# A hybrid decoder step on one core: the one-hot table loaded as 96 rows and one, the key-value state shifted memory to memory

## The chip, the core and the metric

The kernel runs on one core of a Trainium2 chip. The time is what the device reports for one execution, in microseconds (us). The kernel before took 3317.05 us, the median of three runs (3311.76 to 3326.76). The profiled execution from which every row below is taken took 3318.74 us.

Five engines have instruction streams of their own: TensorE (PE, with PEld for its weight loads), VectorE (DVE), ScalarE (ACT), GpSimd (POOL) and SyncE (SP). SP computes nothing here; it issues most of the DMAs. ACT and POOL issue some as well. The transfers themselves run on 16 DMA engines, and a DMA share of 1.00 in the profile means that all 16 are busy.

## The reference, cut to what matters

One step of a decoder layer for a prompt of 1024 tokens and for 8 decode samples. Each token passes a state-space branch and a sparse attention branch, then a mixture of 32 experts. The change touches two places: the bias of the attention by distance, and the sliding-window attention of the 8 samples.

```python
def attend_shared(q, k, v, q_pos, k_pos, mask, table):
    s = jnp.einsum('bhgqd,bkhd->bhgqk', q, k).astype(F32) * HEAD_DIM ** -0.5
    s = s + shared_bias(table, q_pos[:, None] - k_pos[None, :])    # table[rel_bucket(distance)]
    ...
def nsa_sample(...):
    ...
    wkv = jnp.concatenate([win_buf, kv_win], 1)        # 512 old rows and the new one
    ...                                                # attend_window(q, wkv, ...)
# outputs
win_s.append(jnp.concatenate([state_win_kv[l], kvw], 1)[:, -state_win_kv.shape[2]:])
```

`state_win_kv` holds, for each of 8 samples, 512 rows of 256 floats: 128 of keys and 128 of values. The output `win_s` is the same buffer moved up by one row, with the new row at the end; so 511 rows of each sample (523,264 bytes) go from input to output unchanged. The one-hot table `k_onehot` is a constant of 97 rows by 4224 columns in bfloat16 (8448 bytes a row), with which TensorE turns the 32 bias buckets into a bias for each distance.

## The kernel before

The kernel is one program in stages. From 0 to about 430 us the **front** interleaves four strands by a string of letters (ORDER): adaLN (`r`, 24 steps; each loads 1 MB of `w_ada` into one of two `wt` buffers at L499 and multiplies it at L504), the compression of the samples' paged cache (`c`, L1141 to L1166, whose transposes are L1155 and whose products are L475 to L477), the state-space tables (`S`) and the bias tables (`B`, `bias_prep`). Then come the input projections, from about 703 us the prompt attention, from about 1205 us the output projection and routing, from about 1400 us the experts, and from about 3218 us the combination.

**bias_prep** loads the one-hot table `oh` with one DMA from SP's queue (L1240). Its products with the bias table (L1246 to L1271) give the bias for the prompt (`bt`, spread to `bx` by L1250), for the selected blocks, the window and the compressed blocks.

**The prompt attention** (`attention`) walks over 2 head groups and 8 blocks of 128 queries. Between its pieces it takes steps of a second chain, `sample_attention`, at 0.9 steps to a piece; both chains share the in-order queues of PE, DVE and ACT, so a sample step that waits holds up the prompt's work behind it.

**The window part of sample_attention** (L1679 to L1735) takes the samples one by one. `fetch` (L1685) loads a whole 512 KB state with SP into one of two `slab` buffers. For each sample SP stores the slab, moved by a row, to `win_s`: three rows from one partition (L1694) and 508 rows from 127 partitions (L1695). DVE copies the values into `wv` (L1696), PE transposes the keys (L1699), ACT evicts them (L1702), PE multiplies them with the queries (L1705). The buffer of sample b is free for sample b + 2 when its stores have landed. The pool of these tiles opens when the part before it, the selected blocks, has let go of its own: its last reader is L1674.

What sets the order of instructions around the change is a scheduler of the tile framework: within a stage it places each instruction on its engine's queue by the dependencies and by its own estimate of when they are met; the queues are then in order on the chip. DMAs from SP and ACT share eight completion semaphores in turn, and a DMA waits at issue until the earlier one with the same semaphore is done.

Of the kernel before, what the change touches and what calls it, by code (L numbers as in the profile page):

```python
# [10 lines left out]
F = mybir.dt.float32  # L11
# [12 lines left out]
B = 8  # L24
# [426 lines left out]
class K:  # L451
# [763 lines left out]
    def bias_prep(self):  # L1215
        nc, tc, i = self.nc, self.tc, self.i
# [5 lines left out]
        with ExitStack() as c:  # L1222
            p = self.pool("bp", ctx=c)
            q = self.pool("bpq", bufs=2, psum=True, ctx=c)

            tf = p.tile([97, 8], F, name="tf")
            nc.vector.memset(tf[96:97], NEG)
            for k in range(3):
                nc.sync.dma_start(out=tf[32 * k:32 * k + 32], in_=i["rel_bias"])
            tb = p.tile([97, 8], BF, name="tb")  # L1230
            nc.vector.tensor_copy(out=tb, in_=tf)
            t1 = p.tile([96, 8], F, name="t1")
            nc.vector.tensor_tensor(out=t1, in0=tf[0:96], in1=tb[0:96], op=ALU.subtract)
            t2 = p.tile([96, 8], BF, name="t2")
            nc.vector.tensor_copy(out=t2, in_=t1)
            nc.vector.tensor_tensor(out=t1, in0=t1, in1=t2, op=ALU.subtract)
            nc.vector.tensor_copy(out=tb[32:64], in_=t2[32:64])
            nc.vector.tensor_copy(out=tb[64:96], in_=t1[64:96])
            oh = p.tile([97, 4224], BF, name="oh")
            nc.sync.dma_start(out=oh, in_=i["k_onehot"])  # L1240
            bv = p.tile([8, 1152], F, name="bv")
            nc.vector.memset(bv, NEG)
            for a in range(0, 1151, 512):
                n = min(512, 1151 - a)
                po = q.tile([128, 512], F, name="po")[:8]
                nc.tensor.matmul(po[:, :n], lhsT=tb, rhs=oh[:, 3073 + a:3073 + a + n], start=True, stop=True)  # L1246
                nc.vector.tensor_copy(out=bv[:, a:a + n], in_=po[:, :n])
            nc.sync.dma_start(out=self.bt, in_=bv)

            nc.sync.dma_start(out=self.bx, in_=self.bt[:, None].to_broadcast([8, 128, 1152]))  # L1250

            ps = q.tile([128, 512], F, name="po")[:, :256].rearrange("p (a j h) -> p a j h", a=4, j=8)
            for a in range(4):
                for j in range(8):
                    nc.tensor.matmul(ps[:, a, j], lhsT=oh[:, a * 1024 + j:(a + 1) * 1024:8], rhs=tb, start=True, stop=True)
            bs = p.tile([128, 2, 4, 8, 4], F, name="bs")
            for h in range(2):
                nc.vector.tensor_copy(out=bs[:, h], in_=ps[:, :, :, h * 4:h * 4 + 4])
            nc.sync.dma_start(out=self.bsel.rearrange("h a p f -> p h a f"), in_=bs.rearrange("p h a j g -> p h a (j g)"))
            pw = q.tile([128, 512], F, name="po")[:, :32].rearrange("p (j h) -> p j h", j=4)  # L1260
            for j in range(4):
                nc.tensor.matmul(pw[:, j], lhsT=oh[:, 3584 + j:4096:4], rhs=tb, start=True, stop=True)
            bw = p.tile([128, 4, 8], F, name="bw")
            nc.vector.tensor_copy(out=bw, in_=pw)
            nc.sync.dma_start(out=self.bwin, in_=bw)
            t8 = p.tile([97, 8, 8], BF, name="t8")
            nc.vector.tensor_copy(out=t8, in_=tb[:, None, :].to_broadcast([97, 8, 8]))
            pc = q.tile([128, 512], F, name="po")[:64, :256]
            t8 = t8.rearrange("p a b -> p (a b)")
            nc.tensor.matmul(pc[:, 0:255], lhsT=t8, rhs=oh[:, 31:4096:16], start=True, stop=True)  # L1270
            nc.tensor.matmul(pc[:, 255:256], lhsT=t8, rhs=oh[:, 4096:4097], start=True, stop=True)  # L1271
            bc = p.tile([64, 256], F, name="bc")
            nc.vector.tensor_copy(out=bc, in_=pc)
            nc.sync.dma_start(out=self.bcmp, in_=bc)
# [327 lines left out]
    def sample_attention(self, bank):  # L1602
        nc, tc, i = self.nc, self.tc, self.i
        v, A, pe, g_ = nc.vector, nc.scalar, nc.tensor, nc.gpsimd
        self.atts = tc.dram_tile([128, 4, B], F, name="atts")
        lo, hi = half = (slice(0, 64), slice(64, 128))
        ident, keep = self.ident, self.keep
# [4 lines left out]
        with ExitStack() as c:  # L1612
            p = self.pool("sa", ctx=c, side="right")
# [3 lines left out]
            def fetch(k):  # L1617
                w = p.tile([120, 8, 256], F, name="slab", bufs=2)
                g_.indirect_dma_start(out=w.rearrange("p j f -> p (j f)"), out_offset=None, in_=pool, in_offset=off(ap=self.rx[:, 0, k:k + 1], axis=0))
                sb = p.tile([120, 8, 4], F, name="sb", bufs=2)  # L1620
                g_.indirect_dma_start(out=sb.rearrange("p j g -> p (j g)"), out_offset=None, in_=btab, in_offset=off(ap=self.rx[:, 1, k:k + 1], axis=0))
                return w, sb
# [6 lines left out]
            ahead = fetch(0)  # L1629
            ahead += (keys(ahead[0], 0),)  # L1630
            for n in range(4):
                sv = p.tile([120, 4, 8, 64], F, name="sv")
                st = p.tile([120, 8, 4, 4], F, name="st")
                for k in range(4):
                    b, h = divmod(4 * n + k, 2)
                    (w, sb, kw), ahead = ahead, fetch(4 * n + k + 1) if 4 * n + k < 15 else None
                    g_.tensor_copy(out=sv[:, k], in_=w[:, :, 128 + 64 * h:192 + 64 * h])
                    tp = bank(128, 4, 128)
# [13 lines left out]
                for j0 in (0, 4):  # L1652
                    tp = bank(16, 4, 128)
# [24 lines left out]
        with ExitStack() as c:  # L1678
            p = self.pool("saw", ctx=c, side="right")  # L1679
            wv = p.tile([128, B, 4, 128], F, name="wv")  # L1680
# [2 lines left out]
            nc.sync.dma_start(out=bw, in_=self.bwin)  # L1683

            def fetch(b):  # L1685
                w = p.tile([128, 4, 256], F, name="slab", bufs=2)
                nc.sync.dma_start(out=w, in_=i["state_win_kv"][0, b].rearrange("(p j) c h d -> p j (c h d)", j=4))
                return w

            ahead = fetch(0)  # L1690
            for b in range(B):
                w, ahead = ahead, fetch(b + 1) if b < B - 1 else None
                wo = self.o["win_s"][0, b].rearrange("t c h d -> t (c h d)")
                nc.sync.dma_start(out=wo[0:3].rearrange("(p j) f -> p j f", j=3), in_=w[0:1, 1:4])  # L1694
                nc.sync.dma_start(out=wo[3:511].rearrange("(p j) f -> p j f", j=4), in_=w[1:128])  # L1695
                v.tensor_copy(out=wv[:, b], in_=w[:, :, 128:256])  # L1696
                tp = bank(128, 4, 128)
                for j in range(4):
                    pe.transpose(tp[:, j], w[:, j, 0:128], ident)  # L1699
                yield  # L1700
                kt = p.tile([128, 4, 128], F, name="kt")
                A.activation(out=kt, in_=tp, func=AF.Copy)  # L1702
                ws = bank(128, 4, 8)
                for j in range(4):
                    pe.matmul(ws[:, j], lhsT=kt[:, j], rhs=self.qk[:, b], start=True, stop=True)  # L1705
                yield
                v.tensor_tensor(out=wsb[:, :, b], in0=ws, in1=bw, op=ALU.add)
            pw = p.tile([64, 528], F, name="pw")
            tp = bank(64, 4, 128)
# [27 lines left out]
        with ExitStack() as c:  # L1737
            p = self.pool("sac", ctx=c, side="right")
# [577 lines left out]
```

## Time and profile before

| | |
|---|---|
| median of 3 runs | 3317.05 us (3311.76 to 3326.76) |
| profiled execution | 3318.74 us |
| its span | 3316.9 us, so 1.84 us lie around it |
| PE busy | 2963.7 us, 89% |
| DVE busy | 2319.3 us, 70% |
| ACT busy | 1785.9 us, 54% |
| POOL busy | 347.4 us, 10% |
| moved by DMA | 656.34 MB, mean 198 GB/s |

The shares are means over stages with different limits. In the page's line of PE by slices (40 slices of 83 us) a 9 is a slice in which PE hardly rests; the slices to look at are those without. PE idle time counts as waiting when the row names a releaser: "<-DMA slab" means that PE stood until that transfer had landed. PEclk is the clock granted to TensorE, as a share of full speed: 1.00 is 2.4 GHz and 0.50 is 1.2 GHz. DMA is the share of 16 engines, so one engine working alone reads 0.06.

### The profile page before, as it was taken

The page shows a single profiled execution, that of the slowest core. Times are in us where ns is not written, and L with a number is a line of the kernel's source. Part 1 is how long each engine was busy: PE and PEld are TensorE (multiplying, and loading weights), DVE is VectorE, ACT ScalarE, POOL GpSimd, SP SyncE. Part 2 cuts the span into 40 slices and gives each one's busy share as a digit, 9 for nine tenths or more (in the row PEclk, how much of TensorE's full clock was granted, in tenths as well). Part 3 has the DMA queues.
Part 4 walks back from the last instruction along what each step waited for, and adds up shares of the span by engine and source line. Part 5 has one row for each costly group of instructions (what it writes and reads, how often), then busy time and mean ns, then how long its engine had stood idle before and what let it go on. Part 6 is the DMA issues. An engine that isn't in the chain of part 4 may idle for free. (4 is left out here: it accounts for less than half of the span.)

```text
span 3316.9 us, 51065 instructions
## 1 busy us (share of the span) xinstructions
PE 2963.7 (89%) x15681; PEld 2374.8 (72%) x15682; DVE 2319.3 (70%) x4442; ACT 1785.9 (54%) x2824; POOL 347.4 (10%) x451
## 2 busy tenths in 40 slices
PE   6857899998982689769999999999999999999987
PEld 4535699976772458548788888878887888878762
DVE  4734856347871468778978877785579866697878
ACT  2422545456661364346757666574467754575752
POOL 1710121002200000000000000000000000000013
PEclk9978999998995779879999999999999999999988
DMA  7746333223411143289988988892449934694926
GB/s 254 238 164 229 136 111 111 86 72 87 117 45 50 46 161 116 106 295 305 330 279 274 316 284 281 282 319 83 149 158 371 368 125 158 212 363 144 310 96 280
DMA packets 446216, 656.34 MB, mean 198 GB/s; under 512 B 45199, under 2 KB 370816, under 8 KB 442033
## 3 DMA queue, kind: packets, MB, share of 16 engines
q1 hardware_dynamic: 420210, 539.60, 48.5%
q0 software_dynamic: 23184, 111.39, 9.9%
q10 hardware_dynamic: 2704, 3.85, 0.3%
q8 instruction: 64, 1.05, 0.1%
q14 instruction: 54, 0.44, 0.0%
HBM read 590.77 MB, written 68.73 MB: 199 GB/s over the span
## 5 line engine op out<-in xcount | busy, mean ns | idle before, releaser
L272 DVE TENSOR_TENSOR lo<-raw,hi 128x1024 fp32r<-128x1024 f32 x870 | 1030.9, 1222 | 306.9 <-ACT hi L199 301.6
L199 ACT ACTIVATE hi<-raw 128x1024 fp32r<-128x1024 f32 x870 | 916.4, 1060 | 490.6 <-PE pc L388 489.5
L386 PE MATMUL pc<-hi,X 128*128 128x512 f32 x1408 | 560.8, 398 | 4.7 <-DVE X L277 3.8
L388 PE MATMUL pc<-hi,X 128*128 128x512 f32 x1408 | 550.8, 391 | 0.0
L387 PE MATMUL pc<-lo,X 128*128 128x512 f32 x1408 | 549.9, 391 | 0.0
L386 PEld LDWEIGHTS pc<-hi,X 128*128 128x128 f32 x1408 | 265.1, 188 | 60.5 <-issue 8.9
L388 PEld LDWEIGHTS pc<-hi,X 128*128 128x128 f32 x1408 | 264.8, 188 | 56.4
L387 PEld LDWEIGHTS pc<-lo,X 128*128 128x128 f32 x1408 | 265.3, 188 | 51.5
L386 PE MATMUL pc<-hi,HT 128*128 128x512 f32 x704 | 282.7, 402 | 12.1 <-DVE HT L294 9.1
L388 PE MATMUL pc<-hi,HT 128*128 128x512 f32 x704 | 274.7, 390 | 0.0
L387 PE MATMUL pc<-lo,HT 128*128 128x512 f32 x704 | 274.6, 390 | 0.0
L386 PEld LDWEIGHTS pc<-hi,HT 128*128 128x128 f32 x704 | 132.2, 188 | 53.5 <-issue 28.6
L388 PEld LDWEIGHTS pc<-hi,HT 128*128 128x128 f32 x704 | 132.2, 188 | 28.2
L387 PEld LDWEIGHTS pc<-lo,HT 128*128 128x128 f32 x704 | 132.4, 188 | 24.7
L504 PE MATMUL po<-wt,ct 128*9 128x256 f32 x384 | 100.5, 400 | 55.3 <-DMA wt<-in_w_ada_dram 52.6
L475 PE MATMUL po<-wih,hh 128*128 128x256 f32 (+3 forms) x504 | 147.7, 293 | 0.0
L476 PE MATMUL po<-wil,hh 128*128 128x256 f32 (+3 forms) x504 | 147.0, 292 | 0.0
L477 PE MATMUL po<-wih,hl 128*128 128x256 f32 (+3 forms) x504 | 145.9, 289 | 0.0
L1318 DVE CUSTOM_DVE_ANT_0 pt<-sc,tt 128x512 f32<-128x512 f32 (+7 forms) x256 | 107.3, 436 | 52.8 <-PE sc L1334 29.7
L1157 ACT ACTIVATE xh<-tp 128x512 fp32r<-128x512 f32 x128 | 71.3, 595 | 109.2 <-PE tp L1155 101.9
L421 POOL DMA_INDIRECT xg<-hd,ic x52 | 68.2, 1311 | 586.0 <-PE px L354 554.7
L1371 PE MATMUL tp<-ident,pt 128*128 128x128 f32 (+6 forms) x592 | 115.5, 305 | 4.6 <-DVE pt L1357 4.3
(697 smaller groups left out, 5718.6 us busy)
## 6 DMA issues: line engine op xcount, KB each, us to landing
raw<-in_w_gate_up_dram SPq DMA_DIRECT2D x248, 1024.0 KB, 10.1
raw<-in_w_down_dram SPq DMA_DIRECT2D x64, 2048.0 KB
wt<-in_w_ada_dram SPq DMA_DIRECT2D x24, 1024.0 KB
yd<-yt SPq DMA_DIRECT2D x44, 512.0 KB
w<-ssmw SPq DMA_DIRECT2D x16, 512.0 KB
raw<-in_w_gate_up_dram POOLq DMA_DIRECT2D x8, 1024.0 KB, 13.7
wir<-in_w_in_dram SPq DMA_DIRECT2D x20, 256.0 KB
bx<-bt SPq DMA_DIRECT2D x1, 4608.0 KB
```

The source lines that it names most:

```text
L199: A.activation(out=hi[:,u%H],in_=rawview(u),func=AF.Copy).then_inc(S['hi'][u],1)
L272: V.tensor_tensor(out=lo[:,u%H],in0=rawview(u),in1=hi[:,u%H].bitcast(F),op=ALU.subtract).then_inc(S['lo'][u],1)
L386: PE.matmul(o,lhsT=sH,rhs=wh,start=kt==0,stop=False)
L387: PE.matmul(o,lhsT=sH,rhs=wl,start=False,stop=False)
L388: ins=PE.matmul(o,lhsT=sL,rhs=wh,start=False,stop=kt==7)
L475: pe.matmul(o, lhsT=lh, rhs=rh, start=start, stop=False)
L476: pe.matmul(o, lhsT=lh, rhs=rl, start=False, stop=False)
L477: return pe.matmul(o, lhsT=ll, rhs=rh, start=False, stop=stop)
L504: last = nc.tensor.matmul(po, lhsT=ct[:, k], rhs=wt[:, k], start=k == 0, stop=k == KT - 1)
L1157: nc.scalar.activation(out=xo, in_=tp, func=AF.Copy)
L1318: v.tensor_tensor_reduce(out=pt[:, off[r] + a:off[r] + a + n], in0=sc, in1=bias, scale=1.0, scalar=-3e38, op0=ALU.add, op1=ALU.max, accum_ ...
L1371: pe.transpose(tp[:n, h * 128:h * 128 + 128], pr[h][:, a:a + n], self.ident)
```

## The change

Two edits in the code. In `bias_prep` the one-hot table is loaded with two DMAs, rows 0 to 95 and row 96. In the window part the keys and the values are loaded by two DMAs of 256 KB each from POOL's queue, the keys into one of four `slab` buffers and the values straight into `wv`, three samples ahead; the copy on DVE is gone. The shift of the state no longer passes through the chip's memory: one DMA for each sample copies the 511 rows from the input in HBM to the output in HBM, written as 128 pieces of 4088 bytes.

```diff
             oh = p.tile([97, 4224], BF, name="oh")
-            nc.sync.dma_start(out=oh, in_=i["k_onehot"])
+            for a, b in ((0, 96), (96, 97)):
+                nc.sync.dma_start(out=oh[a:b], in_=i["k_onehot"][a:b])
 ...
             def fetch(b):
-                w = p.tile([128, 4, 256], F, name="slab", bufs=2)
-                nc.sync.dma_start(out=w, in_=i["state_win_kv"][0, b].rearrange("(p j) c h d -> p j (c h d)", j=4))
+                w = p.tile([128, 4, 128], F, name="slab", bufs=4)
+                src = i["state_win_kv"][0, b].rearrange("(p j) c h d -> p j c (h d)", j=4)
+                g_.dma_start(out=w, in_=src[:, :, 0])
+                g_.dma_start(out=wv[:, b], in_=src[:, :, 1])
                 return w
 
-            ahead = fetch(0)
+            ahead = [fetch(b) for b in range(3)]
             for b in range(B):
-                w, ahead = ahead, fetch(b + 1) if b < B - 1 else None
-                wo = self.o["win_s"][0, b].rearrange("t c h d -> t (c h d)")
-                nc.sync.dma_start(out=wo[0:3].rearrange("(p j) f -> p j f", j=3), in_=w[0:1, 1:4])
-                nc.sync.dma_start(out=wo[3:511].rearrange("(p j) f -> p j f", j=4), in_=w[1:128])
-                v.tensor_copy(out=wv[:, b], in_=w[:, :, 128:256])
+                w = ahead.pop(0)
+                if b < B - 3:
+                    ahead.append(fetch(b + 3))
+
+                flat = [d[0, b].rearrange("t c h d -> (t c h d)") for d in (self.o["win_s"], i["state_win_kv"])]
+                nc.sync.dma_start(out=flat[0][0:511 * 256].rearrange("(a f) -> a f", a=128), in_=flat[1][256:512 * 256].rearrange("(a f) -> a f", a=128))
                 tp = bank(128, 4, 128)
                 for j in range(4):
-                    pe.transpose(tp[:, j], w[:, j, 0:128], ident)
+                    pe.transpose(tp[:, j], w[:, j], ident)
```

The order moves more than the diff says. On SP's queue around the load of the one-hot table there stands before (`ssmw` is a table of the state-space part, `wt` the adaLN weights, `tf` the bias table, `bx` its spread copy):

```order
L947 DMA ssmw<-wt 128x512
L1229 DMA tf<-in_rel_bias_dram 32x8 x3
L1240 DMA oh<-in_k_onehot_dram 97x4224
L499 DMA wt<-in_w_ada_dram 128x8x256 x5
L1248 DMA bt<-bv 8x1152
L1259 DMA bsel<-bs 128x8x32
L1265 DMA bwin<-bw 128x32
L1274 DMA bcmp<-bc 64x256
L1250 DMA bx<-bt 1024x1x1152
L499 DMA wt<-in_w_ada_dram 128x8x256 x7
```

And on the same queue at the same place now:

```order
L947 DMA ssmw<-wt 128x512
L499 DMA wt<-in_w_ada_dram 128x8x256 x2
L1229 DMA tf<-in_rel_bias_dram 32x8 x3
L1241 DMA oh<-in_k_onehot_dram 96x4224
L499 DMA wt<-in_w_ada_dram 128x8x256
L1241 DMA oh<-in_k_onehot_dram 1x4224
L1700 DMA out_dram<-in_state_win_kv_dram 16x8176
L499 DMA wt<-in_w_ada_dram 128x8x256
L1700 DMA out_dram<-in_state_win_kv_dram 16x8176
L499 DMA wt<-in_w_ada_dram 128x8x256 x2
L1700 DMA out_dram<-in_state_win_kv_dram 16x8176
L1249 DMA bt<-bv 8x1152
```

The thirteenth load of `wt`, first behind the table before, now stands ahead of it. The copies of the state (L1700) wait for no computation, and so the scheduler has pulled all eight out of the window part into the front: four before the table, three here and one after `bx`. The compiler has folded the 128 pieces of each into 16 rows of 8176 floats (32,704 bytes).

On SP's queue at the start of the window part there stood before:

```order
L1683 DMA bw<-bwin 128x32
L1687 DMA slab<-in_state_win_kv_dram 128x1024 x2
L1694 DMA out_dram<-slab 1x768
L1695 DMA out_dram<-slab 127x1024
L1694 DMA out_dram<-slab 1x768
L1695 DMA out_dram<-slab 127x1024
L1687 DMA slab<-in_state_win_kv_dram 128x1024 x2
```

On POOL's queue, where the loads stand now (the first row is the last work for the selected blocks):

```order
L1627 COPY kw<-slab 120x512
L1689 DMA slab<-in_state_win_kv_dram 128x4x128
L1690 DMA wv<-in_state_win_kv_dram 128x4x128
L1689 DMA slab<-in_state_win_kv_dram 128x4x128
L1690 DMA wv<-in_state_win_kv_dram 128x4x128
L1689 DMA slab<-in_state_win_kv_dram 128x4x128
L1690 DMA wv<-in_state_win_kv_dram 128x4x128
L1689 DMA slab<-in_state_win_kv_dram 128x4x128
```

The loads and stores of the window have left SP; POOL issues 16 loads, and behind them on its queue stands nothing until the output projection. A third place is the front from about 120 to 150 us, again SP's queue; before (each `ssmw` and `ssmk` is a store that waits for DVE, ACT or POOL):

```order
L933 DMA ssmw<-v_1036 128x4x128
L927 DMA ssmw<-o_1031 128x2x512
L499 DMA wt<-in_w_ada_dram 128x8x256
L941 DMA ssmk<-kt 16x4x128
L947 DMA ssmw<-wt 128x512
```

Now:

```order
L933 DMA ssmw<-v_1036 128x4x128
L927 DMA ssmw<-o_1031 128x2x512
L1700 DMA out_dram<-in_state_win_kv_dram 16x8176
L941 DMA ssmk<-kt 16x4x128
L947 DMA ssmw<-wt 128x512
L927 DMA ssmw<-o_1068 128x2x512
L933 DMA ssmw<-v_1073 128x4x128
L941 DMA ssmk<-kt 16x4x128
L947 DMA ssmw<-wt 128x512
L933 DMA ssmw<-v_1110 128x4x128
L499 DMA wt<-in_w_ada_dram 128x8x256
```

A copy has taken the place of the ninth `wt` load, which now stands behind seven more stores.

## Rows read from the trace of the kernel before

**Rows 1.** The page's second part: PE and DMA in 40 slices, tenths.

```profile
PE   6857899998982689769999999999999999999987
DMA  7746333223411143289988988892449934694926
```

**Rows 2.** Waits of PE, 180 to 330 us: total, times, longest.

```profile
PE po L504 <- DMA wt<-in_w_ada_dram: 51.4, 2, 34.0
```

**Rows 3.** Waits of PE, 960 to 1140 us.

```profile
PE b L1699 <- DMA slab<-in_state_win_kv_dram: 95.3, 4, 33.7
```

**Rows 4.** Waits of SP's queue, 960 to 1140 us.

```profile
SPq L1687 <- DMA out_dram<-slab: 76.7, 6, 13.6
```

**Rows 5.** Stretches: us, busy PE, PEld, DVE, ACT, POOL, PEclk, DMA share, GB/s.

```profile
200.00:216.00 16.00, 0.00 (x0) 0.00 (x0) 0.00 (x0) 0.00 (x0) 0.00 (x0) 0.50 0.06 27
256.00:264.00 8.00, 8.00 (x54) 5.64 (x54) 3.77 (x8) 2.79 (x6) 1.12 (x2) 1.00 1.07 428
281.00:292.00 11.00, 9.96 (x68) 7.16 (x67) 6.53 (x12) 4.25 (x9) 1.04 (x2) 1.00 0.53 209
...
720.00:980.00 260.00, 239.13 (x1505) 188.04 (x1504) 202.86 (x787) 172.43 (x409) 52.14 (x64) 0.90 0.33 80
980.00:1135.00 155.00, 58.88 (x293) 48.09 (x293) 40.07 (x158) 37.52 (x85) 0.00 (x0) 0.64 0.13 48
```

**Rows 6.** DMA issues: count, KB each, median us to landing where known.

```profile
bx<-bt SPq DMA_DIRECT2D x1, 4608.0 KB
...
out_dram<-slab SPq DMA_DIRECT2D x8, 508.0 KB
...
oh<-in_k_onehot_dram SPq DMA_DIRECT2D x1, 800.2 KB
...
sel<-in_k_sel_dram POOLq DMA_DIRECT2D x1, 256.0 KB, 3.0
```

**Rows 7.** SP's queue around the one-hot table and `bx`: start, us, operation.

```profile
180.69 0.29 SPq L1240 DMA_DIRECT2D oh<-in_k_onehot_dram  x1
...
189.94 27.48 SPq L499 DMA_DIRECT2D wt<-in_w_ada_dram  x1
...
289.69 21.09 SPq L499 DMA_DIRECT2D wt<-in_w_ada_dram  x1
```

**Rows 8.** PE's timeline, 183 to 230 us, the adaLN products.

```profile
184.01 1.46 PE L504 MATMUL po<-wt,ct 128*9 128x256 f32 x6
...
225.31 2.72 PE L504 MATMUL po<-wt,ct 128*9 128x256 f32 x6 [34.04 <-DMA wt<-in_w_ada_dram]
```

**Rows 9.** PE's timeline, 308 to 320 us.

```profile
317.40 3.16 PE L504 MATMUL po<-wt,ct 128*9 128x256 f32 x7 [17.38 <-DMA wt<-in_w_ada_dram]
```

**Rows 10.** PE's timeline in the window part.

```profile
974.39 1.09 PE L1674 MATMUL b<-st,sv 120*64 120x4 f32 x16
...
980.57 0.66 PE L1699 MATMUL b<-ident,slab 128*128 128x128 f32 x4 [1.21 <-DMA slab<-in_state_win_kv_dram]
...
1024.31 1.09 PE L1699 MATMUL b<-ident,slab 128*128 128x128 f32 x4 [33.74 <-DMA slab<-in_state_win_kv_dram]
...
1027.02 0.78 PE L1331 MATMUL sc<-kh,qs 128*128 128x512 f32 x1
...
1036.87 0.48 PE L1331 MATMUL sc<-kh,qs 128*128 128x512 f32 x1
```

**Rows 11.** Three stretches after the window's waits: columns of rows 5; first, and sum.

```profile
1024.30:1034.90 10.60, 10.55 (x39) 8.72 (x40) 7.44 (x30) 5.72 (x12) 0.00 (x0) 0.50 0.17 63
...
sum 29.30, PE 29.21 PEld 25.18 DVE 19.02 ACT 15.17 POOL 0.00; mean PE 9.74 PEld 8.39 DVE 6.34 ACT 5.06 POOL 0.00
```

**Rows 12.** POOL's loads of the selected blocks: ns min/median/max, and landing in us.

```profile
L1619 POOL DMA_INDIRECT slab<-in_cache_sel_kv_dram,rx x16: 971/987/1102, 766.4 to 933.2; - x16
...
DMA to landing us min/median/max: 7.6/8.0/12.8
```

**Rows 13.** DVE's groups by form, 700 to 1200 us.

```profile
L1357 DVE TENSOR_SCALAR pt<-pt,sm 128x1024 f32<-128x1024 f32 x8 | 6.1, 769 | 0.0
...
L1696 DVE COPY wv<-slab 128x512 f32<-128x512 f32 x8 | 3.4, 424 | 97.2 <-DMA slab<-in_state_win_kv_dram 97.2
```

## The prediction

> **What bounds the kernel now.** I read the page's slices first, then the waits of the engine that is busiest, then the stretches in which it stands. PE is at 8 or 9 in most slices of 83 us. Two places fall out: the first five (the front, to 415 us), lowest in the third with 5, and the thirteenth and fourteenth (995 to 1161 us) with 2 and 6, where DMA stands at 1 [rows 1]. Neither PE nor the DMA engines as a whole limit the second place. The waits tell what does: in the window part PE stood 95.3 us for slabs [rows 3], and SP's next slab loads stood 76.7 us for the stores from the slabs [rows 4]. In the front PE stood 51.4 us in two waits for `wt` [rows 2].
>
> The width of the transfers explains both. From 200 to 216 us the share is 0.06, one sixteenth, at 27 GB/s, with PE at zero; from 281 to 292, while `bx` is written, it is 0.53 at 209 GB/s; in a stretch of `wt` and cache loads it is 1.07 at 428 GB/s [rows 5]. So one DMA engine gives about 27 GB/s, and the one-hot table, of 97 rows, ran on one, `bx` on eight. 800.2 KB (819 kB) at 27 GB/s are 30.3 us. Each store from 127 partitions, 508.0 KB [rows 6] (520 kB), takes 19.3 us in the same way, a pair 38.5 us, with two slab buffers to wait for: that is the rhythm of the window's waits.
>
> **The change part by part.** *Window stores.* The stretch from 980 to 1135 us holds the eight samples: 155 us. Of the 95.3 us of waits 1.2 are the first slab's [rows 3, 10]; 94.1 come from the stores, and go. What is left is 155 - 94.1 = 60.9 us. Of this 29.3 us, three stretches after the three long waits, ran at a granted clock of 0.50, 1.2 GHz [rows 11]; the same matmul takes 0.78 us there and 0.48 later [rows 10], a ratio of 1.6, so at 2.4 GHz they would take 18.3: 49.9 us of work at full clock. The attention before this place ran at a mean of 0.90 [rows 5], that is a fifth of its time at the lower level: 49.9 / (0.8 + 0.2/1.6) = 53.9 us. Two checks: DVE did 40.07 us of work in the stretch, 3.4 of it the eight copies of values that go [rows 13]; at its rate before (202.86 of 260) the rest needs 47 us; ACT's 37.52 at its rate (172.43 of 260) need 57 [rows 5]. I take 53.9; the ends are 47 and 57.
>
> *Window loads.* Sixteen loads on POOL. The nearest issue is the indirect load of the blocks, 0.99 us [rows 12]: at most 16 us in a stretch in which POOL is at 0.00 [rows 5]. The three first fetches wait for the last reader of the old pool, which starts at 974.39 [rows 10] and ends at about 975.5, as SP's did. Nearest landings: 3.0 us for 256 KB from POOL [rows 6] and 8.0 for the large indirect loads [rows 12]; PE wants the first keys some seven order rows earlier than before, near 978. So the first three slabs cost 1 to 10 us together; I take 5, near the 3.0 us of the row of the same size, with three fetches queued in a burst. From the fourth on a fetch is three to four samples ahead, at 53.9 / 8 = 6.7 us a sample 20 us or more, which hides even a landing of 12.8 us [rows 12]; without that cover it is the first rival. So 155 becomes 53.9 + 5 - 1.2 = 57.7, a saving of 97 us; between 88 (57 and 10 us) and 108 (47 and no wait).
>
> The Trainium skill has a rule against this edit, in SBUF — State Buffer, section "SBUF: two separate sides": a DMA issued from POOL has its descriptors written by that engine, and stands while VectorE runs an fp32 copy that takes both port pairs; it gives 620 ns alone and about 3100 ns beside such a copy. By those figures eight key loads would each come 2.5 us later, an estimate of 20 us if PE waited for each, and the time 3214. The operations it speaks of are in this stage (DVE's scaling of 1024 floats in 769 ns [rows 13]); but beside a DVE that is busy 78% of the time the issues of POOL took 971 to 1102 ns [rows 5, 12], so the trace bears it out by a tenth of a microsecond at the issue and perhaps in the spread of landings.
>
> *One-hot table.* 96 rows on 16 engines are 811 kB at 428 GB/s, 1.9 us in place of 30.3. The single row of 8.4 kB is 0.3 us on one engine, at a place in the queue where the first loads of `wt` no longer wait for it. In the trace the second load behind the table was held at its issue for 27.48 us [rows 7], and PE stood 34.04 us for the first [rows 8]. Now that first load, the thirteenth, is ahead of the table. It goes out when PE has finished the eleventh, at 184.01 + 1.46 = 185.5 [rows 8], and PE wants it at 225.31 - 34.04 = 191.3, 5.8 us later. A `wt` that nothing held lands 6.6 us after its issue ends (289.69 + 21.09 = 310.8 to 317.40 [rows 7, 9]). So 0.8 us remain, with a little for the queue 2: 32 of the 34 us go. The products behind the wait run at the lower clock, 2.72 us for the six that took 1.46 [rows 8]; some 5 us of work were slowed so, which gives back 2.
>
> *The eight copies, now in the front.* 523 kB each, from HBM to HBM. The nearest row is `bx`, which is also written from HBM to HBM and moves at the common rate of one engine times eight [rows 5]; on 16 engines a copy is 1.2 us, eight 10 us, on SP's queue between the loads of `wt`. Between the table's wait and the one behind `bx` PE never stood for a `wt` [rows 2], so the two buffers leave time to spare, and cover a copy; I put 3 us on the path. Without that cover it is 10, with luck 0.
>
> *Order in the front.* The ninth and tenth `wt` now stand behind stores that wait for DVE, close to the products that need them. If each is late by its whole landing, 2 x 6.6 = 13 us; if DVE is ahead, 0. I take 4, nearer to 0, because PE waits for DVE itself in that part.
>
> *The second wait, 17.38 us* [rows 9], follows `bx`, which is unchanged with a load of `wt` behind it; it stays.
>
> The front saves 32 + 2 - 3 - 4 = 27 us; between 4 (34 - 6.6 - 10 - 13) and 36 (all of 34, and 2 for the clock).
>
> *The sum.* 3318.74 - 97 - 27 = 3195 for the profiled execution, which lies 1.7 us above the median of the runs shown; I take **3194**. Nothing behind the two places absorbs it: PE is at 9 in what follows but for two slices at the change to the experts [rows 1], and the loads of those stages wait for memory that the stage before frees, so they move with it.
>
> **The rivals.** *A: the keys come late from POOL.* Each fetch lands as late as the worst in the trace, 12.8 us, 4.8 over the median, and PE waits for it all eight times: 38 us, 3194 + 38 = 3232. For it: 512-byte pieces in place of 4 KB, and POOL's queue is in order, a fetch behind another. Against it: the distance of four buffers.
>
> *B: the front gives nothing.* The reordered loads and the copies cost as much as the table's stall gave back: 3194 + 27 = 3221. For it: DMA is at 7 in the first two slices [rows 1], where four copies go. Against it: of the two waits for `wt` in the front, one was this table's.
>
> *C: slower.* The copies run on one engine, as the table and the 127-partition stores did. Then each is 523 kB / 27 GB/s = 19.4 us, in the one place where every load of `wt` shares that engine's queue, and holds SP at its issue as the table held it [rows 7]. Eight of them are 155 us in the path of the front: 3194 + 155 = 3349. It decides from 124 / 8 = 15.5 us a copy. Against it: loads cut into 128 partitions ran wide, at 428 GB/s [rows 5], and 16 rows of 8176 can be dealt out evenly as they are, which 127 and 97 cannot.
>
> **How the numbers follow.** The forecast has 0.74; its own range, from the ends of both places, is 3318.74 - 108 - 36 = 3175 to 3318.74 - 88 - 4 = 3227. A has 0.09, B 0.13, C 0.04. The likeliest reaches to B; with A taken in by most of its part the range is 3175 to 3230, which leaves out C, half of A and the tails of the forecast, some 0.16. About 0.5%, 17 us, is what a measurement of this kernel can tell from no change. Faster by more than that are the forecast, A and B, 0.96, less 0.01 for gains lost in both places at once, which I give to no change: 0.95 and 0.01. Slower is C, 0.04.
>
> **What would show it.** In the window part no wait of PE for `slab` longer than about 5 us, a stage of 55 to 60 us, and a mean clock near 0.90. No stretch at a share of 0.06 with PE at zero, neither near 190 us nor there; a wait of a few us for the thirteenth `wt`; the 17 us wait behind `bx` still there. Each copy in a microsecond or two at a high share, and no `wt` issue held for tens of us other than behind `bx`. Wrong would be PE waits of 4 us or more for every slab (A), new waits for the ninth and tenth `wt` or around the copies (B), or a row of stretches at 27 GB/s in the front (C).

## The result and the profile after

The changed kernel took 3207.85 us, the median of four runs (3204.67 to 3217.46), against 3319.23 us for the kernel before, measured beside it (four runs, 3311.76 to 3326.76). The ratio is 0.966, with a 95% interval of 0.963 to 0.969. Forecast were 3194 us and a range of 3175 to 3230. On a second chip the same kernel gave 0.965 (0.963 to 0.968). The profiled execution of after took 3209.21 us, 109.5 less than that of before; 124 were forecast.

The page's slices of after (columns as in [rows 1]):

```profile
PE   7787899998999898599999999999999999999977
PEclk9888899988879799699999999999999999999988
DMA  8766343223512342798979869764289915792926
```

The 2 and 6 of PE in the thirteenth and fourteenth slices of before are gone; in after they read 9 and 8 (a slice of after is 80 us). The slabs no longer appear among PE's waits there, where 95.3 us stood [rows 3], and in the front the two waits of 51.4 us [rows 2] have become 26.0. The waits of PE in after, first from 180 to 330 us, then from 940 to 1095 us:

```profile
PE po L504 <- DMA wt<-in_w_ada_dram: 26.0, 2, 16.5
...
PE tp L1372 <- DVE pt L1358: 2.1, 1, 2.1
PE po L1377 <- DVE at L1388: 1.7, 2, 1.1
```

One number must be set aside before the two profiles are subtracted. The profile of before began with a wait of 20.0 us of PE for its first loads, that of after with one of 8.8 us. This belongs to the execution: a second profile of the changed kernel (the last run below) has 20.3 us there, other kernels have 9.1 or about 20 to 21. So stretches are counted from the first product behind that wait. What is left of it is small: in the two profiles with the short wait (after, and after without copies) PE then stands 3.5 to 3.9 us for the first `wt`, and in the others under 2 us, so their fronts read some 3 us longer. Each ends at the start of a named product in the timeline of PE: the first scores of the prompt attention, the first transpose of a window slab, the first transpose for the output projection (`tpg`), the last single product of all.

| us | before | after | after, second profile |
|---|---|---|---|
| front and input projections, to the first scores | 680.2 | 670.6 | 667.5 |
| attention ahead of the window | 276.2 | 288.2 | 287.2 |
| window and the rest of the attention | 235.0 | 130.4 | 130.7 |
| projection, routing, experts, combination | 2080.6 | 2084.6 | 2081.3 |

So the window gave 105 us and the front 10 to 13; the attention between them took 11 to 12 back, and the stages behind 1 to 4.

Stretches of after (the columns are those of [rows 5]; the attention ahead of the window is cut in three, then the eight samples, up to the first transpose of the window's softmax weights, L1725 here and L1721 before, then the rest of the attention):

```profile
683.60:853.60 170.00, 153.66 (x917) 119.95 (x916) 132.85 (x570) 113.57 (x298) 32.23 (x41) 0.87 0.33 81
853.60:893.60 40.00, 34.95 (x188) 28.44 (x188) 27.59 (x102) 24.16 (x50) 12.40 (x14) 0.83 0.62 156
893.60:971.80 78.20, 75.69 (x450) 62.15 (x451) 49.89 (x180) 43.14 (x98) 11.73 (x16) 0.74 0.15 37
971.80:1020.50 48.70, 46.76 (x302) 37.97 (x300) 40.36 (x162) 37.79 (x88) 8.66 (x12) 1.00 0.25 82
1020.50:1102.20 81.70, 71.19 (x436) 56.56 (x435) 49.72 (x219) 50.45 (x155) 1.79 (x7) 0.80 0.17 55
```

The last two stretches of before, between the same products:

```profile
980.50:1136.10 155.60, 59.54 (x295) 48.39 (x295) 41.03 (x158) 38.62 (x90) 0.00 (x0) 0.64 0.13 47
1136.10:1215.60 79.50, 69.96 (x436) 54.70 (x435) 49.16 (x218) 49.14 (x154) 1.77 (x7) 0.81 0.21 65
```

The samples run at a granted clock of 1.00 with PE busy 46.76 of 48.70 us; before it was 0.64, and 155.60 us for about the same number of products. So they gave 107 us, and the rest of the attention took 2 back. Of the 12 us lost ahead of the window most go in the third row: at the same place before, the clock was 0.90 and the stretch took 66.2 us.

```profile
874.40:914.40 40.00, 35.59 (x212) 28.74 (x210) 31.61 (x112) 26.93 (x56) 13.19 (x16) 0.91 0.62 156
914.40:980.60 66.20, 61.98 (x441) 50.82 (x440) 48.66 (x180) 40.85 (x94) 8.15 (x11) 0.90 0.19 48
```

(These two are of the kernel before, cut at the same distances from its first scores. Counted product by product, in an order that is nearly the same, after is 3 us behind where the third row begins and 12 where it ends.) In the front the wait of 34.04 us before the thirteenth step's products [rows 8] is gone, and two are new: 7.03 us before the ninth step and 9.55 us before the twelfth. PE's rows of after at both, then the queues ahead of them, and the stretches between the first load and the first row:

```profile
144.18 5.65 PE L504 MATMUL po<-wt,ct 128*9 128x256 f32 x16 [7.03 <-DMA wt<-in_w_ada_dram]
...
198.90 5.58 PE L504 MATMUL po<-wt,ct 128*9 128x256 f32 x16 [9.55 <-DMA wt<-in_w_ada_dram]
```

```profile
127.71 0.36 SPq L933 DMA_DIRECT2D ssmw<-v  x1
128.17 0.46 SPq L499 DMA_DIRECT2D wt<-in_w_ada_dram  x1
...
191.91 0.36 SPq L927 DMA_DIRECT2D ssmw<-o  x1
192.37 0.42 SPq L947 DMA_DIRECT2D ssmw<-wt  x1
192.88 1.72 SPq L499 DMA_DIRECT2D wt<-in_w_ada_dram  x2
```

```profile
127.72 0.98 POOL L1141 DMA_INDIRECT raw<-in_cache_cmp_kv_dram,ix  x1 [4.07 <-DVE rr L1151]
...
131.74 0.97 POOL L1141 DMA_INDIRECT raw<-in_cache_cmp_kv_dram,ix  x1 [0.83 <-DVE rr L1151]
```

```profile
128.00:133.00 5.00, 3.70 (x28) 3.33 (x28) 3.52 (x6) 0.98 (x2) 4.14 (x5) 1.00 0.96 304
133.00:139.00 6.00, 2.74 (x12) 1.55 (x12) 2.55 (x5) 2.24 (x5) 3.17 (x4) 0.64 1.01 430
139.00:144.20 5.20, 0.03 (x1) 0.03 (x2) 1.93 (x2) 0.00 (x0) 3.90 (x3) 0.50 0.94 330
```

PE had come to the two at 137.15 and 189.35 (the start of the products less the wait). The two waits have different causes. The products at 198.90 are the twelfth step; their load left directly behind two stores of the state-space tables at 192.88, when PE already stood, and landed 6 us later. The products at 144.18 are the ninth step. Their load left at 128.17 (118.4 in before), in time for PE if it had landed in the 5 to 8 us of a load by itself. But two cache loads of POOL left beside it, at 127.72 and 131.74, the DMA engines were at a share of 0.94 to 1.01, and it landed after 16 us. In before no cache load left between 113 and 150 us.

### The profile page after: what moved, and what is told of

Its sections match the earlier page's. It is cut to its first block, busy times and chain, and to the rows that moved or that the text cites. A ratio compares the mean times of both kernels' runs of the same rounds, so it can differ in the third digit from the quotient of the medians.

```text
span 3207.4 us, 51067 instructions
## 1 busy us (share of the span) xinstructions
PE 2972.0 (93%) x15681; PEld 2380.6 (74%) x15682; DVE 2321.0 (72%) x4434; ACT 1785.9 (56%) x2824; POOL 358.7 (11%) x467
## 5 line engine op out<-in xcount | busy, mean ns | idle before, releaser
L386 PE MATMUL pc<-hi,X 128*128 128x512 f32 x1408 | 561.0, 398 | 4.7 <-DVE X L277 3.8
L386 PEld LDWEIGHTS pc<-hi,X 128*128 128x128 f32 x1408 | 265.2, 188 | 60.6 <-issue 8.9
L386 PE MATMUL pc<-hi,HT 128*128 128x512 f32 x704 | 282.6, 401 | 12.1 <-DVE HT L294 9.0
L386 PEld LDWEIGHTS pc<-hi,HT 128*128 128x128 f32 x704 | 132.2, 188 | 53.4 <-issue 28.5
```

What stands on the lines that cost most here:

```text
L386: PE.matmul(o,lhsT=sH,rhs=wh,start=kt==0,stop=False)
```

## The experiments

All times are against the kernel before on the same chip. The table gives the stretches as above (front; attention ahead; window and rest; all behind), from one profile each.

| kernel | ratio, 95% interval | front | ahead | window | behind |
|---|---|---|---|---|---|
| before | 1 | 680.2 | 276.2 | 235.0 | 2080.6 |
| after | 0.966, 0.963-0.969 | 670.6 | 288.2 | 130.4 | 2084.6 |
| table split alone | 0.990, 0.988-0.992 | 645.6 | 289.4 | 229.0 | 2080.6 |
| window part alone | 0.973, 0.971-0.974 | 692.3 | 284.0 | 130.6 | 2081.3 |
| stores 112 + 15 alone | 0.972, 0.970-0.975 | 678.6 | 274.1 | 130.9 | 2093.6 |
| after, no copies | 0.959, 0.957-0.961 | 649.3 | 287.1 | 125.5 | 2083.0 |
| no copies, loads held | 0.961, 0.959-0.964 | 659.1 | 287.5 | 130.8 | 2083.3 |
| copies behind table | 0.965, 0.962-0.968 | 661.0 | 287.0 | 130.7 | 2080.9 |
| copies in window | 0.967, 0.965-0.969 | 645.3 | 284.4 | 140.0 | 2094.8 |
| the same, bx wide | 0.961, 0.959-0.964 | 633.3 | 289.7 | 136.8 | 2095.8 |
| loads on SP | 0.964, 0.961-0.966 | 669.5 | 284.9 | 129.8 | 2081.5 |
| two splits | 0.963, 0.961-0.965 | 642.4 | 288.8 | 130.7 | 2097.7 |
| two splits, bx wide | 0.961, 0.958-0.963 | 638.5 | 285.4 | 133.2 | 2095.0 |

**The parts alone.** First the table's split in the kernel before:

```diff
-            nc.sync.dma_start(out=oh, in_=i["k_onehot"])
+            for a, b in ((0, 96), (96, 97)):
+                nc.sync.dma_start(out=oh[a:b], in_=i["k_onehot"][a:b])
```

> The kernel before with the one-hot table split into 96 rows and one, and nothing else. My theory: the table's split alone takes away nearly all of the 34 us wait, and what the front of the changed kernel gave less than that was spent by the eight copies and the order that came with them. Then the time is 3319 - 27 = about 3292 (3285 to 3297), and the wait for the thirteenth wt is under 6 us. Rival: the wait would have come back anyway, because the loads of wt stand behind the stores of the state-space tables; then a wait of about 10 us stays there, as in the changed kernel, and the time is 3305 or more.

Measured 3290.66 us, 0.990. The front became 34.6 us shorter, where the changed kernel's gained 10 to 13. Of the waits for `wt` the one behind `bx` stayed, and one of 1.1 us. PE's waits for `wt` in this kernel, from 30 to 440 us:

```profile
PE po L504 <- DMA wt<-in_w_ada_dram: 19.3, 2, 18.2
```

The theory holds, and the rival, a wait of 10 us behind the stores, does not show here. Then the window part, with the table in one piece:

```diff
-            for a, b in ((0, 96), (96, 97)):
-                nc.sync.dma_start(out=oh[a:b], in_=i["k_onehot"][a:b])
+            nc.sync.dma_start(out=oh, in_=i["k_onehot"])
```

> The changed kernel with the one-hot table loaded in one piece of 97 rows again. My theory: the window part alone is worth about 105 us in its place, loses some 15 us behind it, and the table on one engine costs its 34 us wait again: 3208 + 25 = about 3233 (3225 to 3240). Rival: the front gave nothing by the table, since copies and order in the front fill whatever it frees; then 3208 to 3215. A third possibility is that the table on one engine holds the copies behind it too: 3245 or more.

3236.67 us, 0.973, as the first theory has it. The front is 12 us longer than before, 22 to 25 longer than in the two profiles of after. The window stands at 130.6. Last, the kernel before with its stores split, all else as it was (whole slabs from SP, two buffers, the copy on DVE):

```diff
-                nc.sync.dma_start(out=wo[3:511].rearrange("(p j) f -> p j f", j=4), in_=w[1:128])
+                for a, b_ in ((1, 113), (113, 128)):
+                    nc.sync.dma_start(out=wo[4 * a - 1:4 * b_ - 1].rearrange("(p j) f -> p j f", j=4), in_=w[a:b_])
```

> The kernel before with each store of 127 partitions written as one of 112 and one of 15, and nothing else: loads of whole slabs by SP, two buffers and the copy by DVE stay. My theory: the width of the store alone made the window's waits; a store of 112 partitions takes about 1 to 2 us on 16 engines, so the three waits of 34 us fall to a few us each, and the time is 3319 - 90 = about 3230 (3222 to 3240). Rival: a slab's round trip (load, wait, store, wait, two buffers) still holds each sample by its landings, some 5 to 8 us for each pair: 3250 to 3265.

3228.27 us, 0.972. One line gives the whole of the window's gain: 130.9 us against 130.4 with loads apart, four buffers, POOL and copies. PE's longest wait from 975 to 1040 us is not for a slab, and the eight samples (with more of the prompt's products between them than in after) run at a clock of 1.00:

```profile
PE sc L1331 <- DVE mx L1318: 1.0, 1, 1.0
```

```profile
977.80:1033.30 55.50, 53.35 (x338) 42.59 (x338) 47.77 (x188) 43.74 (x104) 0.00 (x0) 1.00 0.46 145
```

In before, while a store from 127 partitions ran and PE stood, the share was that of one engine:

```profile
990.00:1000.00 10.00, 0.57 (x2) 0.18 (x1) 0.00 (x0) 0.77 (x4) 0.00 (x0) 0.73 0.06 27
```

So the width of the store was the cause, and neither the way through the chip's memory nor the number of buffers was.

**Whether POOL's queue matters.**

```diff
-                g_.dma_start(out=w, in_=src[:, :, 0])
-                g_.dma_start(out=wv[:, b], in_=src[:, :, 1])
+                nc.sync.dma_start(out=w, in_=src[:, :, 0])
+                nc.sync.dma_start(out=wv[:, b], in_=src[:, :, 1])
```

> The changed kernel with the sixteen loads of keys and values issued by SP instead of POOL, in the same places; nothing else moves. Theory: with four buffers the issuing queue does not matter, since PE waits for no slab in the changed kernel: within 0.002 of the changed kernel's ratio of 0.966, and the drop of the granted clock before the window (0.80 between 880 and 960 us) is there too. Rival: POOL's issues (about 1 us each) or their slower landings cost something that the waits don't show, or SP's stores of the attention output stand behind waiting slab loads: 0.963 or less in the first case, 0.969 or more in the second.

3208.04 us, 0.964 (0.961 to 0.966), where after has 0.966 and 0.965 on two other chips: the intervals overlap, and the window is the same within 1 us. The queue does not matter, as far as these runs can tell.

**What the copies cost.** The changed kernel without its eight copies:

```diff
-                nc.sync.dma_start(out=flat[0][0:511 * 256].rearrange("(a f) -> a f", a=128), in_=flat[1][256:512 * 256].rearrange("(a f) -> a f", a=128))
```

> The changed kernel without the eight copies of the state, so win_s is left without its 511 old rows. My theory: the copies, and the order of the wt loads that they bring, cost the front about 15 to 18 us (the 7 us and 10 us waits for wt of the changed kernel go back to 2 or 3 us each); 3208 - 15 = about 3193 (3188 to 3198). Rival: the copies are free (1.2 us each on 16 engines, beside other work) and the two waits stay: 3203 to 3210.

3187.56 us, 0.959. The front is 21 us shorter than that of after (both profiles begin with the short wait), more than I expected, and of the waits the one behind `bx` is left and one of 3.4 us for the first `wt`. PE's waits for `wt` from 30 to 440 us, in the second profile of after and then here:

```profile
PE po L504 <- DMA wt<-in_w_ada_dram: 36.0, 4, 17.0
```

```profile
PE po L504 <- DMA wt<-in_w_ada_dram: 21.2, 2, 17.8
```

There is a second loss, PE's clock. The stretch from the first product to the wait behind `bx`, the same 1384 products, in after and then without copies:

```profile
13.10:280.60 267.50, 221.85 (x1384) 157.13 (x1384) 168.54 (x339) 93.03 (x182) 76.79 (x70) 0.92 0.71 253
```

```profile
13.40:256.90 243.50, 214.57 (x1384) 153.82 (x1384) 164.26 (x339) 94.46 (x183) 77.36 (x70) 0.98 0.75 261
```

221.85 us of busy PE against 214.57, at 0.92 and 0.98. Up to `bx` after has lost 24 us to the kernel without copies (some 3 come back later); 16.6 of them are the two waits, and 7 are PE's longer busy time (in the second profile of after it is 217.66, 3 longer). Is it the copies' bytes, or the order into which they push the `wt` loads? One run has the order without copies: four loads of `wt` are tied behind the stores where after has them.

```diff
+            hold = {8: (12, 1), 9: (12, 0), 10: (12, 3), 11: (28, 3)}.get(n)
+            with self.tc.issue_after(self.stored[hold].ins) if hold else ExitStack():
                 nc.sync.dma_start(out=wt, in_=i["w_ada"][0].rearrange("(k p) f -> p k f", p=128)[:, :, s])
```

> The kernel without copies once more (win_s is left without its 511 old rows), with the ninth to twelfth loads of wt tied behind the stores of the state-space tables, about where they stand in the changed kernel. It has the order without the traffic. Theory (order): waits for wt of 5 to 10 us come back before the ninth and the twelfth or thirteenth products, and the front is 15 to 20 us longer than without copies: ratio 0.964 to 0.966 against 0.9592. Rival (traffic): the waits came from the copies' bytes and issues, and without them the front stays as it was: 0.958 to 0.961.

3200.29 us, 0.961 (0.959 to 0.964), between the two expectations, and its interval overlaps that without copies. The long waits that the theory of order foretold did not come: those for `wt` add up to 3.7 us beside the one behind `bx`. But the front is 10 us longer than without copies, and that is PE's busy time at a clock of 0.93, for the same 1384 products:

```profile
PE po L506 <- DMA wt<-in_w_ada_dram: 20.9, 4, 17.2
```

```profile
24.30:279.10 254.80, 224.56 (x1384) 159.69 (x1384) 166.42 (x339) 95.47 (x184) 78.22 (x70) 0.93 0.67 234
```

The order is not quite that of after: in after PE's queue has the 16 products of a whole step in a row at both waits, here those of the ninth to eleventh step stand in groups of 2 to 10 between others. The other run keeps the copies in the front, but behind the table:

```diff
+                with self.tc.issue_after(self.oh_load.ins):
                     nc.sync.dma_start(out=flat[0][0:511 * 256].rearrange("(a f) -> a f", a=128), in_=flat[1][256:512 * 256].rearrange("(a f) -> a f", a=128))
```

> The changed kernel with its eight copies tied behind the load of the one-hot table: they stay in the front, each between two loads of wt, but the wt loads up to the table stand in SP's queue as they do without copies. It tells the order from the traffic. Theory (order): the two waits of 7 and 10 us for wt are gone, and the copies' 1.2 us each add at most 6 us: ratio 0.959 to 0.963. Rival (traffic): every copy holds the wt load behind it by its issue and its bytes, eight times about 3 us, and the ratio stays at 0.965 to 0.968.

3208.92 us, 0.965, its front at 661.0. The waits for `wt` are gone as the theory has it, but others came: 8.8 us for `mt` and, later, 11.5 us for `rr`, both for DVE, whose queue had been reordered as well. PE's waits in the front:

```profile
PE po L504 <- DMA wt<-in_w_ada_dram: 17.5, 2, 16.6
PE tp L605 <- DVE rr L602: 11.5, 1, 11.5
PE po L504 <- DVE mt L508: 11.0, 5, 8.8
```

These two profiles begin with the long wait, the one without copies with the short one. Three kernels of the table with no copies in the front (table alone, copies in window, two splits) begin with the long wait and have PE's, DVE's and POOL's instructions in the same order there as the kernel without copies. Their fronts take 642.4 to 645.6 us. Against these the held loads cost 14 to 17 us, the copies behind the table 15 to 19, and the changed kernel in its second profile 22 to 25.

So neither pure theory stands. By the fronts the order by itself, without a byte of the copies, costs more than half of what the copies do; by the ratios it is a third (0.961 between 0.959 and 0.966), with an interval that holds both. Each place of the copies gives a new order on several queues. How much of the rest their bytes alone cost stays open.

**The copies in the window part, and a wider `bx`.**

```diff
-            nc.sync.dma_start(out=bw, in_=self.bwin)
+            first = nc.sync.dma_start(out=bw, in_=self.bwin)
 ...
+                with self.tc.issue_after(first.ins):
                     nc.sync.dma_start(out=flat[0][0:511 * 256].rearrange("(a f) -> a f", a=128), in_=flat[1][256:512 * 256].rearrange("(a f) -> a f", a=128))
```

> The changed kernel with its eight copies tied behind the load of bw on SP's queue, so that they are issued in the window part instead of the front; everything is computed. Without the copies the kernel took 0.9592 of before. Theory: the copies cost what they cost (0.9662 against 0.9592, some 23 us) because of where they stand in the front, not by their traffic; in the window part the DMA engines have room. Ratio 0.959 to 0.962 (about 3185 to 3192 where before takes 3319). Rival: 8.4 MB moved costs its time anywhere, because the keys' loads stand beside it: 0.964 or more.

3215.67 us, 0.967: no gain, against the theory. The front did become what it is without copies (645.3). But the window and the rest of the attention lost 10 us, and the stages behind 10 to 14, on which more below. The copies run beside the slab loads, but that is not where the 10 us went: the eight samples took 50.4 us in place of 48.7, with 1.5 us of waits for slabs, and the rest of the attention, in which no copy runs, 89.6 in place of 81.7. There PE waited 7.6 us for one step of DVE, where after has 1.7. Why is open. That wait, then SP's issue of five copies and a stretch in which they run and no slab load does:

```profile
PE po L1377 <- DVE at L1388: 7.6, 2, 5.8
```

```profile
970.92 3.04 SPq L1701 DMA_DIRECT2D out_dram<-in_state_win_kv_dram  x5
...
972.00:978.00 6.00, 5.82 (x38) 5.00 (x39) 4.74 (x17) 4.49 (x12) 0.76 (x1) 1.00 1.02 338
```

A share near 1 says that the copies do use all 16 engines. The second kernel adds one line:

```diff
-            nc.sync.dma_start(out=self.bx, in_=self.bt[:, None].to_broadcast([8, 128, 1152]))
+            nc.sync.dma_start(out=self.bx.rearrange("h p f -> p h f"), in_=self.bt[None].to_broadcast([128, 8, 1152]))
```

> The same as the kernel with late copies, and the spread of the bias table (bx) written with 128 as its outermost dimension instead of 8; everything is computed. Theory: bx ran on 8 of 16 DMA engines because of that dimension (209 GB/s, 22 us for 4608 KB); on 16 it takes 11 us, and the wait of about 17 us behind it falls to about 7: 10 us, or 0.003 of the time, below the kernel with late copies. Rival: the wait is the length of a chain bt, bx, wt, each of which waits for the last one's landing, and it falls by less than 3 us; the two kernels are then equal within 0.001.

3202.46 us, 0.961, 0.0056 below the other; 0.003 was expected. PE's wait behind `bx` fell from 17.8 to 10.0 us, and the front by 12. Share and rate in the wait behind `bx`, of this kernel (262 to 268 us), then of after (288 to 292 us):

```profile
262.00:268.00 6.00, 1.75 (x15) 1.54 (x14) 0.43 (x1) 0.88 (x2) 0.00 (x0) 0.86 1.02 427
```

```profile
288.00:292.00 4.00, 0.00 (x0) 0.00 (x0) 0.00 (x0) 0.00 (x0) 0.00 (x0) 0.50 0.53 216
```

**A better kernel.** The two splits, in the kernel before, and nothing else (the diffs of the first and third experiment):

> The kernel before with two splits and nothing else: the one-hot table as 96 rows and one, the store of 127 partitions as 112 and 15. Everything is computed. Theory: the two places are independent and no copy burdens the front, so the gains add: 0.9898 + 0.9724 - 1 = 0.962 (0.959 to 0.965), about 3194 where before takes 3319; that is below the changed kernel's 0.966. Rival: what one place gains the other loses through the clock, and it stays at 0.966 or above.

3204.71 us, 0.963 (0.961 to 0.965). The sum of the parts, 0.962, holds, and the front keeps all of its gain; but "behind" is 13 to 16 us longer than in the two profiles of after. With the `bx` line as well:

> The same with bx written with 128 as its outermost dimension. Everything is computed. Theory: 8 to 11 us less than without it (the wait behind bx falls from 17 to about 9), so a ratio of about 0.959 (0.955 to 0.961). Rival: the products that stand behind that wait then wait for something else, and it gains under 3 us.

3197.02 us, 0.961 (0.958 to 0.963); the wait fell to 9.8 us as expected, and the gain of 0.002 is within the intervals. Beside both ran the changed kernel:

> The changed kernel as it is, beside the two on the same chip: 0.966 of before, as measured. Its profile tells whether the first wait of PE (8.8 us for fold in the profile of the changed kernel, 20.0 in that of the kernel before) belongs to the kernel or to the execution: I expect either value.

3213.73 us, 0.965 (0.963 to 0.968). The two splits with the wide `bx`, three small edits, are 16.7 us below the changed kernel by the medians on one chip; the intervals just overlap, so it is at least as good and probably better.

## Why the prediction was right, and where its sum was off

*The window's stores.* Right. The waits for slabs went, and the split of the stores alone shows the mechanism. For the stage of the eight samples 57.7 us were forecast, and it took 48.7. The clock's term was too careful: I carried the 0.90 of the attention before into a stage that then ran at 1.00; 53.9 us at 0.90 are 49.9 at full clock. This is 4 of the 9 us, and the price of the first slabs, 5, which was not paid, is most of the others. The rest of the attention took 2 back, and 105 us came where 97 were forecast, within the range of 88 to 108.

*The window's loads.* The price of 5 us for the first slabs was not paid: PE waited for none. POOL issued the eight key loads in 747 to 800 ns each (below the 0.99 us of [rows 12]), and rival A falls with it:

```profile
L1703 PE MATMUL b<-ident,slab x32: 270/272/273, 971.8 to 1008.5; 128*128 128x128 f32 x32
...
L1689 POOL DMA_DIRECT2D slab<-in_state_win_kv_dram x8: 747/748/800, 968.2 to 991.3; - x8
```

(Columns: duration min/median/max in ns, first and last start.) The rule of the Trainium skill against such loads (SBUF — State Buffer, "SBUF: two separate sides": descriptors written by POOL wait for VectorE's two-port copies) gave an estimate of 20 us; with loads from SP the window was 129.8 us against 130.4, so no run here shows it where buffers are loaded three samples ahead.

*The table.* Right by itself: 32 us and 2 of the clock were forecast, 34.6 came in the run with this edit alone. In after PE does not wait for the thirteenth load either.

*Copies and order in the front.* This is the step that was mis-sized: "I put 3 us" and "I take 4", seven in all, where the runs without copies in the front show 21 to 25. The ends that the prediction gave, 10 and 13, about hold it. The reason for 4 was that DVE would be ahead, since PE waits for DVE in that part. For the twelfth load the rows of SP show the reverse: it left behind stores whose data DVE and ACT had just made, and PE was already there (9.55 us). The ninth left 10 us later than before and took 16 us to land, beside two cache loads of POOL (7.03 us); the prediction counted 6.6 us for a landing, whatever ran beside it. I had looked at the queue that issues, and not at POOL's, nor at PE's own, which had been reordered with it and wants a whole step in a row. The lower clock, 7 us of busy time in one profile and 3 in the other, was left out too. And the 6.6 us were read from two rows that do not belong together:

```profile
279.10 31.68 SPq L499 DMA_DIRECT2D wt<-in_w_ada_dram  x2
```

The products at 317.40 wait for the first of these two loads, and the one at 289.69 is the second. That other loads of that trace landed in about as long (5.1 to 7.5 us for the eighth, the tenth to twelfth and the fifteenth) is luck.

*The second wait,* 17.38 us [rows 9], stayed: 16.5 and 17.0. Writing `bx` with 128 outermost shows that its width, too, was a part of it.

*"Nothing behind the two places absorbs it."* Wrong by 12 to 16 us: 11 to 12 in the attention between them, 1 to 4 behind. Rival C is out (five copies, alone, ran at a share of 1.02); rival B was half true, since the front gave 10 to 13 us of its 27.

The sum of the first two profiles, from the first product on: -9.6 + 12.0 - 104.6 + 4.0 = -98.2, and -11 by the start, which the second profile of after doesn't have. Of the 109.5 us by which the profiled execution fell, 11 are thus not the change's: with the long wait in both profiles it is 105.

## What to carry to other kernels

Look first for transfers that run on few engines (127 and 97 rows on one, a leading 8 on eight): a share of 0.06 or 0.53 beside an idle PE names them, and splitting one line can be worth all that a rebuilt stage is. A DMA without inputs to wait for floats to the front of its queue and moves its neighbours there, on other engines' queues too; look where it lands, what it pushes behind a store and which loads it brings together, before calling its bytes cheap. Count what the clock gives back or takes at every wait that comes or goes.

## What the runs showed that I had not expected

The attention ahead of the window lost 8 to 14 us in every kernel whose front was changed (284.0 to 289.7), and none where it was not (276.2 and 274.1), in one profile each: the same work, in nearly the same order, at a granted clock of 0.83 to 0.85 over the stretch in place of 0.88 or 0.89. About half of it or more falls behind 255 us after the first scores, where the clock drops to 0.50; only the two splits with the wide `bx` lose it earlier, from 120 us on. The front's length is not the cause, since the window part alone has a longer front and the loss (284.0); the cause is open.

Five kernels (the stores alone, both with late copies, both with two splits) took 12 to 15 us longer in the experts (1775 to 1776 us from the first expert product, L386, to the start of the last of that line, where all others took 1762 to 1763), whose instructions on PE and DVE stand in the same order in all. There DVE waits for itself longer, a little in each expert, and PE for it. The rows over most of the expert stage of the two splits, then of the changed kernel in its second profile (busy, mean ns of one, idle before and releaser):

```profile
L386 PE MATMUL pc<-hi,HT 128*128 128x512 f32 x688 | 276.4, 402 | 22.6 <-DVE ut L293 11.5 <-DVE HT L294 11.0
L293 DVE SCALAR_TENSOR_TENSOR ut<-st,ut 128x256 f32<-128x256 f32 (+1 forms) x143 | 76.6, 536 | 37.7 <-DVE ut L293 33.8 <-ACT st L222 2.1
```

```profile
L386 PE MATMUL pc<-hi,HT 128*128 128x512 f32 x688 | 276.4, 402 | 12.4 <-DVE HT L294 9.2 <-DVE ut L293 1.9 <-issue 0.2
L293 DVE SCALAR_TENSOR_TENSOR ut<-st,ut 128x256 f32<-128x256 f32 (+1 forms) x143 | 76.6, 536 | 29.5 <-DVE ut L293 25.4 <-ACT st L222 2.4
```

Nothing in the edits touches that stage. The changed kernel has it in neither of its two profiles; the others have one profile each, so that it belongs to the kernel and not to the execution is likely and not shown, and what sets it is open. Without it the two splits would have gained some 13 us more.
